# Attention's entry of a diffusion backbone step: first value tiles unit by unit, the exp table loaded ahead, background products three block steps later, and a later spread in one norm chain

## The chip, the cores and the metric

One NeuronCore of a Trainium2 chip runs the whole program. The metric is the device time of one execution in microseconds (us). The engines in the text are PE (TensorE, the matmuls), DVE (VectorE), ACT (ScalarE), POOL (GpSimd) and SP, which issues most of the DMAs.

## The reference, cut to what matters

Two layers work on 640 tokens of width 1024: 512 latent tokens and 128 context tokens. Each layer is a half-step SwiGLU FFN, a token mixer and another half-step FFN. The mixer of layer 0 is a Fourier mix, that of layer 1 is 16-head attention. Every sub-layer has an RMS norm in front and one behind, with shift, scale and gate from a modulation product.

```python
def _rmsnorm(x, g):
    x32 = x.astype(jnp.float32)
    y = x32 * lax.rsqrt(jnp.mean(x32 * x32, axis=-1, keepdims=True) + RMS_EPS)
    return (y * g.astype(jnp.float32)).astype(x.dtype)
def _modulation(cond, w_mod, b_mod):
    m = jax.nn.silu(cond) @ w_mod + b_mod
    return m.reshape(cond.shape[0], N_MOD, D_MODEL)
def _half_ffn(x, m, k, g_pre, g_post, w1, w2):
    h = _modulated_prenorm(x, g_pre, m, k)
    return x + 0.5 * m[:, 3 * k + 2, None] * _rmsnorm(_swiglu(h, w1, w2), g_post)
def _context_attention(q, k, v):
    s = jnp.einsum('bhqd,bhkd->bhqk', q, k).astype(jnp.float32)
    p = jax.nn.softmax(s, axis=-1).astype(v.dtype)
    return jnp.einsum('bhqk,bhkd->bhqd', p, v)
...
        logits = jnp.concatenate([s_loc.reshape(b, h, GRID_W, n_loc), s_ctx], axis=-1)
        p = jax.nn.softmax(logits, axis=-1).astype(v.dtype)
```

## The kernel before

Tokens lie along the free dimension and are worked in two halves of 320; channels lie on the 128 partitions in 8 chunks. The six sub-layers are numbered n = 0 to 5: FFN, Fourier mix, FFN, FFN, attention, FFN. Every product with a weight matrix is three matmuls (`mm3`, L226 to L232): each operand is split into a high and a low part, and high by high, high by low and low by high are added in one PSUM bank. A weight tile (a "unit" of 128 x 1024) is sent by one DMA into a raw buffer; ACT makes its high part (L195) and DVE its low part (L196). There are four raw buffers and six for high and low parts together.

PSUM holds four "main" banks, two "score" banks, one "turn" and one "sum" bank. The two score banks matter here: the first value tiles are accumulated in them, and the attention scores afterwards.

The order on each engine is fixed when the program is built. The code keeps a clock of its own: each `mm3` advances it (`tick`, L234), and side chains (norms, the residual additions) are generators that yield a delay and are resumed when that clock has passed it. `behind_of` (L219) and `high_priority` move an instruction in the builder's order. Each engine then works in its order; what the semaphores hold back holds back all that is behind it on that engine.

A norm chain (`inverse_rms`, L454) adds the two squares (L461, DVE), takes the mean over the channels on PE (L470), adds eps on DVE (L474), takes the power -1/2 on POOL (L475), yields `root` (2200), and spreads the result over the partitions on PE (L480); ACT copies that from PSUM. `pre` (L490) then multiplies (L505), applies shift and scale (L511 on DVE, L513 on ACT) and splits the result into the two parts of the hidden tile.

Attention's entry (`attention`, L1087 to L1104) runs while the norm of the second half is still in its chain. It takes the products of the first half (two queries, two keys), then the first two value tiles of head quad 1 and of quad 0, then the products of the second half. A value tile is 8 chunks of 3 matmuls with 256 columns; a quad has two weight units, `v0` for chunks 0 to 3 and `v1` for chunks 4 to 7. `v_tiles` (L1031) finishes one token tile before it begins the next; `v_out` (L1027) copies each finished bank to two value buffers on DVE.

`attend` (L1131) makes a list of 40 block steps, plus two to drain, that are woven into the products. One step holds the scores of a block (L1154 on PE, then one DVE instruction that adds the bias and takes the extreme, L1157, then the exponential with its sum on ACT, L1140, and a reciprocal on DVE, L1141), the scaling of the block before (L1174, ACT), its transposes (L1181, PE) and copies (L1183, ACT), and the product with the values of the one before that (L1197, PE). At every third step from 0 to 33 it also takes one job from the background: a DMA of 512 KB of the modulation matrix, and two weighted sums of it on DVE (`gemv`, L389).

Of the kernel before, what the change touches and what calls it, by code (L numbers as in the profile page):

```python
# [14 lines left out]
AF = mybir.ActivationFunctionType  # L15
# [5 lines left out]
NCH = D // P  # L21
# [89 lines left out]
class Kernel:  # L111
# [378 lines left out]
    def pre(self, layer, sub, half, acc=None, fold=1800):  # L490

        nc = self.nc
        n = layer * 3 + sub
        h = self.hs[n]
        if acc is None:
            for c in range(0, NCH, 2):
                acc = self.sum_square(acc, self.xpair(n, c, half))
        r = yield from self.inverse_rms(acc, fold=fold)
        self.normed[half][1] = True
        rb = r[:, :HALF].unsqueeze(1)  # L500
        high = self.tc.high_priority
        for c in range(0, NCH, 2):
            with high() if c == 0 else ExitStack():
                t = self.pair(self.y, c, half)
                nc.vector.tensor_tensor(t, self.xpair(n, c, half), rb.to_broadcast([P, 2, HALF]), op=ALU.mult)  # L505
                for i in (c, c + 1):
                    for s, e, cond in SEGS[half]:
                        k = self.coef[:, layer, sub, :, cond, i : i + 1]
                        t = self.y[:, i, s:e]
                        if i % 2:  # L510
                            nc.vector.tensor_scalar(t, t, k[:, 1], k[:, 0], op0=ALU.mult, op1=ALU.add)  # L511
                        else:
                            nc.scalar.activation(t, t, AF.Identity, bias=k[:, 0], scale=k[:, 1])  # L513
                self.ready = self.split(h.at(0, c, half, 2), h.at(1, c, half, 2), self.pair(self.y, c, half))
            yield 2200
# [431 lines left out]
    def attention(self, base, boundary):  # L947
        nc, io = self.nc, self.io
# [3 lines left out]
        at = {key: base + n for n, key in enumerate(QKV_ORDER)}  # L952
        early = {key: base + QKV_ORDER.index(key) for key in QKV_ORDER}
# [53 lines left out]
        def double(c):  # L1007

            with self.tc.high_priority():
                for p0, (rows, other) in enumerate(sides):  # L1010
                    k = pairs[c][1 + p0]
                    nc.vector.tensor_copy(k[other], k[rows])
# [12 lines left out]
        def v_out(quad, t, ps):  # L1025
            for i, v in enumerate(values[quad]):
                nc.vector.tensor_copy(v[:, t, :], ps[:, i * P : (i + 1) * P])  # L1027
                if t == 4:
                    nc.sync.dma_start(out=io["v_out"][2 * quad + i], in_=v[:, t, :])

        def v_tiles(quad, ts, at=at, bank="main"):  # L1031
            if quad not in values:
                kind = ("total", "square")[quad % 2]
                values[quad] = [self.temp(kind).rearrange("p (t d) -> p t d", t=5) for _ in range(2)]
            w = [self.unit(at["v0", quad]), self.unit(at["v1", quad])]
            for t in ts:
                ps = self.bank(bank)
                for kk in range(NCH):
                    a = [self.h.tokens(part, kk, t * P, (t + 1) * P) for part in range(2)]
                    ww = w[kk // 4]  # L1040
                    ws = slice((kk % 4) * 256, (kk % 4) * 256 + 256)
                    self.mm3(ps[:, :256], a[0], a[1], ww[0][:, ws], ww[1][:, ws], kk == 0, kk == NCH - 1)
                v_out(quad, t, ps)

        def products(jobs, half=None):


            todo = []
            for job in jobs:
                if job[0] == "v":  # L1050
                    quad, t = job[1:]
                    todo.append((self.bank("score"), [self.unit(early["v0", quad]), self.unit(early["v1", quad])], t))
                else:
                    todo.append((self.bank(), self.unit(early[job]), None))
            for k in range(NCH):
                for ps, w, t in todo:
                    if t is None:
                        a = k * P
                        self.mm3(ps[:, :HALF], w[0][:, a : a + P], w[1][:, a : a + P], *self.h.chunk(k, half),
                                 k == 0, k == NCH - 1)  # L1060
                    else:
                        a = [self.h.tokens(part, k, t * P, (t + 1) * P) for part in range(2)]
                        ws = slice((k % 4) * 256, (k % 4) * 256 + 256)
                        self.mm3(ps[:, :256], *a, w[k // 4][0][:, ws], w[k // 4][1][:, ws], k == 0, k == NCH - 1)

            def put(part=slice(None)):
                with self.tc.high_priority():
                    for job, (ps, w, t) in list(zip(jobs, todo))[part]:
                        if t is None:
                            {"q": query, "k": key}[job[0]](job[1], half, ps)  # L1070
                        else:
                            v_out(job[1], t, ps)
            return put
# [8 lines left out]
        for quad in (1, 0):  # L1082
            while not self.normed[1][1 - quad]:
                self.step(1)
            if quad == 0:
                with self.behind_of(self.summed, self.squared):
                    put(slice(2))  # L1087
            v_tiles(quad, (0, 1), early, "score")
        self.finish(1)
        with self.behind_of(*self.ready):  # L1090
            for c in (0, 1):
# [1 line left out]
            put(slice(2, 4))  # L1093
        with self.behind_of(self.latest):
            put = products([("k", 0), ("q", 0), ("v", 0, 3), ("v", 0, 4)], 1)
        put(slice(1))
        double(0)
        put(slice(1, None))
        v_tiles(0, (2,), early, "score")
        plan = {0: (1, (2, 3, 4)), 2: (2, (0, 1)), 3: (2, (2, 3, 4)), 4: (3, (0, 1)), 5: (3, (2, 3, 4))}  # L1100
        for c in range(NCH - 1):
            quad, ts = plan.get(c, (0, ()))
            self.weave(period(c), (qk_ns if c else qk_ns / 2) + len(ts) * v_ns)
            if c in (3, 5):  # L1104
                v_tiles(quad, ts)
            if c:
                qk(c + 1)
            else:
                for which, put in (("k", key), ("q", query)):
                    ps = self.proj(self.unit(early[which, 1]), lambda kk: kk * P, 1)  # L1110
                    with self.tc.high_priority():
                        put(1, 1, ps)
                    if which == "k":
                        double(1)
            if ts and c not in (3, 5):
                v_tiles(quad, ts)
            self.flush()
# [13 lines left out]
    def attend(self, pairs, ctx_qk, v):  # L1131
# [3 lines left out]
        nc, io = self.nc, self.io  # L1135
# [72 lines left out]
        for n in range(len(blocks) + 2):  # L1208
            parts = []
            if 1 <= n <= len(blocks):  # L1210
                parts.append(partial(scale, *blocks[n - 1]))
            if n < len(blocks):
                c, b = blocks[n]
                parts += [partial(ctx_scores if b == "c" else scores, c, b, p0) for p0 in range(2)]
            if n >= 2:
                parts.append(partial(take, *blocks[n - 2]))
            if 1 <= n <= len(blocks):
                parts += [partial(turn, *blocks[n - 1], p0) for p0 in range(2)]
            if n < 35 and n % 3 == 0:
                parts.append(self.behind)  # L1220
            steps.append(parts)
        return steps
# [143 lines left out]
```

## Time and profile before

| What | us |
|---|---|
| time, median of 3 runs (lowest to highest) | 2284.67 (2283.75 to 2285.11) |
| the profiled execution's own time | 2284.21 |
| its span | 2282.4 |
| PE busy in it | 2246.8 |
| DVE busy in it | 1731.9 |
| ACT busy in it | 1270.8 |

The span runs from the first instruction to the last of the profiled execution; the 1.8 us between it and that execution's time lie outside. Busy times of different engines overlap. The rows from the trace give a start time within the span, a duration, the engine, the line, the operation with its output and input, and in square brackets how long the engine had been idle and what ended that. Matmuls are pipelined: the start of one to the start of the next is what one costs.

### The profile page before, as it was taken

What the parts mean: (1) busy time and instruction counts of PE and PEld (TensorE: products, weight loads), DVE (VectorE), ACT (ScalarE), POOL (GpSimd) and SP (SyncE); (2) the same over time, 40 slices, a digit from 0 to 9 for tenths busy, and PEclk for the clock granted to TensorE, in tenths of its full rate; (3) what the DMA queues carried; (4) which work ended last, traced back from release to release, by engine and by line L of the source; (5) the groups of instructions that cost most, each with busy time, mean ns of one, the idle gap of its engine ahead of it and who ended that gap; (6) DMA issues with size and microseconds to landing.
All of it is one profiled execution on the core that took longest, in us unless ns stands there. A gap on an engine that the chain in (4) does not pass through costs nothing.

```text
span 2282.4 us, 39296 instructions
## 1 busy us (share of the span) xinstructions
PE 2246.8 (98%) x15666; PEld 2209.4 (97%) x15666; DVE 1731.9 (76%) x3009; ACT 1270.8 (56%) x2466; POOL 42.8 (2%) x64
## 2 busy tenths in 40 slices
PE   7999999999999999999999999999999999999998
PEld 5999999999999999999999999998998999999997
DVE  5889888588788887867878888587667485766674
ACT  5445545565654545556445554577778654545544
POOL 0000000000000000000000000000000000000000
PEclk8999999999999999999999999999999999999999
DMA  8244443433323433443234443424333222322322
GB/s 306 93 130 157 151 138 118 148 94 123 121 105 118 148 114 127 134 162 112 85 128 140 157 130 104 147 92 141 111 110 113 70 73 100 111 93 80 105 90 96
DMA packets 80280, 278.12 MB, mean 122 GB/s; under 512 B 8800, under 2 KB 15200, under 8 KB 79968
## 3 DMA queue, kind: packets, MB, share of 16 engines
q1 hardware_dynamic: 78736, 273.97, 36.4%
q8 instruction: 122, 2.00, 0.4%
q10 hardware_dynamic: 1360, 1.64, 0.2%
q14 instruction: 62, 0.51, 0.1%
HBM read 264.04 MB, written 11.53 MB: 121 GB/s over the span
## 4 chain that ended last, share of the span: by engine, by line
PE 96%; DVE 2%; DMA 1%; ACT 1%; issue 0%; POOL 0%; DVEq 0%; SPq 0%; ACTq 0%
PE main L229 28%; PE main L231 27%; PE main L230 27%; PE score L230 3%; PE score L229 3%; PE score L231 3%; PE sum L1197 1%; PE score L1154 1%; PE sum L470 1%; PE sum L480 1%; PE turn L1181 1%; DMA first<-in_w_mod_k 0%; PE main L1181 0%; DMA ring<-in_x 0%; DVE lo L196 0%
## 5 line engine op out<-in xcount | busy, mean ns | idle before, releaser
L229 PE MATMUL main<-ring,hi 128*128 128x320 f32 x3872 | 1206.4, 312 | 1.5 <-ACT ring L366 1.1
L231 PE MATMUL main<-ring,lo 128*128 128x320 f32 x3872 | 1198.2, 310 | 0.0
L230 PE MATMUL main<-ring,hi 128*128 128x320 f32 x3872 | 1198.0, 309 | 0.0
L229 PEld LDWEIGHTS main<-ring,hi 128*128 128x128 f32 x3872 | 727.9, 188 | 7.2 <-issue 3.3
L230 PEld LDWEIGHTS main<-ring,hi 128*128 128x128 f32 x3872 | 728.1, 188 | 0.8 <-issue 0.3
L231 PEld LDWEIGHTS main<-ring,lo 128*128 128x128 f32 x3872 | 727.9, 188 | 0.6 <-issue 0.5
L195 ACT ACTIVATE hi<-raw 128x1024 fp32r<-128x1024 f32 (+1 forms) x366 | 356.0, 974 | 434.6 <-PE main L230 354.4
L196 DVE TENSOR_TENSOR lo<-raw,hi 128x1024 fp32r<-128x1024 f32 (+1 forms) x366 | 408.9, 1118 | 143.9 <-ACT hi L195 142.6
L389 DVE SCALAR_TENSOR_TENSOR junk<-raw,wide 128x1024 bf16<-128x1024 f32 x256 | 312.9, 1222 | 20.1 <-DMA raw<-in_w_mod_t 17.3
L698 ACT ACTIVATE y<-main 128x320 f32<-128x320 f32 x318 | 135.5, 431 | 149.4 <-PE main L231 148.6
L672 ACT ACTIVATE main<-y 128x320 f32<-128x320 f32 x256 | 111.5, 439 | 39.1 <-DVE left L654 27.3
L229 PE MATMUL score<-ring,hi 128*128 128x320 f32 x416 | 128.7, 309 | 0.0
L230 PE MATMUL score<-ring,hi 128*128 128x320 f32 x416 | 128.5, 309 | 0.0
L231 PE MATMUL score<-ring,lo 128*128 128x320 f32 x416 | 128.5, 309 | 0.0
L425 DVE TENSOR_TENSOR total<-total,square 128x640 f32<-128x640 f32 x71 | 58.4, 824 | 83.3 <-ACT square L424 81.9
L196 DVE TENSOR_TENSOR lo<-sums,hi 128x1024 fp32r<-128x1024 f32 x72 | 88.0, 1222 | 42.1 <-ACT hi L195 41.2
L195 ACT ACTIVATE hi<-sums 128x1024 fp32r<-128x1024 f32 x72 | 76.3, 1060 | 33.6 <-DVE sums L181 19.3
L229 PE MATMUL main<-ring,ring 128*128 128x320 f32 x288 | 90.9, 316 | 0.0
L231 PE MATMUL main<-ring,ring 128*128 128x320 f32 x288 | 89.1, 310 | 0.0
L230 PE MATMUL main<-ring,ring 128*128 128x320 f32 x288 | 89.0, 309 | 0.0
L229 PEld LDWEIGHTS score<-ring,hi 128*128 128x128 f32 x416 | 78.1, 188 | 0.0
L230 PEld LDWEIGHTS score<-ring,hi 128*128 128x128 f32 x416 | 78.1, 188 | 0.0
(191 smaller groups left out, 2599.6 us busy)
## 6 DMA issues: line engine op xcount, KB each, us to landing
raw<-in_w SPq DMA_DIRECT2D x264, 512.0 KB, 3.6
raw<-in_w_mod_t SPq DMA_DIRECT2D x128, 512.0 KB, 4.2
raw<-in_qkv SPq DMA_DIRECT2D x26, 512.0 KB, 3.7
first<-in_w_mod_k SPq DMA_DIRECT2D x16, 512.0 KB, 9.2
spill<-ring SPq DMA_DIRECT2D x12, 640.0 KB, 3.3
ring<-spill SPq DMA_DIRECT2D x12, 640.0 KB, 7.0
raw<-in_bias SPq DMA_DIRECT2D x16, 448.0 KB, 3.4
raw<-in_four_in SPq DMA_DIRECT2D x8, 512.0 KB, 6.5
```

Of the source, the lines that this page charges most:

```text
L195: nc.scalar.activation(hi, raw[:, at], AF.Copy)
L196: nc.vector.tensor_tensor(lo, raw[:, at], hi.bitcast(F32), op=ALU.subtract)
L229: mm(out, whi, xhi, start=start, stop=False)
L230: mm(out, whi, xlo, start=False, stop=False)
L231: self.latest = mm(out, wlo, xhi, start=False, stop=stop)
L389: last = self.nc.vector.scalar_tensor_tensor(out=self.junk, in0=raw, scalar=1.0, in1=self.wide[:, cond, :], op0=ALU.mult, op1=ALU.mult, ac ...
L425: nc.vector.tensor_tensor(acc, acc, sq, op=ALU.add)
L470: nc.tensor.matmul(ps[:, j : j + 1], part[:, t : t + P], self.mean, start=i == j == 0 or len(acc) == 1, stop=i == len(acc) - 1, skip_group ...
L480: self.spread = nc.tensor.matmul(ps[:, t : t + P], col[:, j : j + 1].to_broadcast([P, P]), self.ident, start=True, stop=True)
L672: nc.scalar.activation(ps[:, :HALF], self.y[:, m, lo:hi], AF.Copy)
L698: nc.scalar.activation(self.y[:, m, lo:hi], ps[:, :HALF], AF.Copy)
L1154: nc.tensor.matmul(o, q, k[:, BLOCK_KEYS[b]], start=part == 0, stop=part == 1)
```

## The change

It has four parts. First, `pre` asks for the spread of one norm chain later: for the second half of sub-layer 3 (layer 1's first FFN) `root` is 3800 in place of 2200 of the code's own clock. Second, the first value tiles of quad 1 are taken unit by unit: chunks 0 to 3 of both token tiles, then chunks 4 to 7 of both, each `mm3` placed behind the one before it; both score banks are open meanwhile. Third, an exponential of one column, whose result nothing reads, is placed on ACT after the products of the second half, ahead of the copies that follow. Fourth, the background jobs go to block steps 3, 6, ... 36 in place of 0, 3, ... 33.

```diff
@@ pre
-        r = yield from self.inverse_rms(acc, fold=fold)
+        r = yield from self.inverse_rms(acc, 3800 if half and n == 3 else 2200, fold)
@@ v_tiles
-        def v_tiles(quad, ts, at=at, bank="main"):
+        def v_tiles(quad, ts, at=at, bank="main", by_unit=False):
...
-            for t in ts:
-                ps = self.bank(bank)
-                for kk in range(NCH):
+            pss = {}
+            for t, kks in ((t, kks) for kks in ((range(4), range(4, NCH)) if by_unit else (range(NCH),)) for t in ts):
+                ps = pss[t] = pss.get(t) or self.bank(bank)
+                for kk in kks:
...
-                    self.mm3(ps[:, :256], a[0], a[1], ww[0][:, ws], ww[1][:, ws], kk == 0, kk == NCH - 1)
-                v_out(quad, t, ps)
+                    with self.behind_of(*[self.latest] if by_unit else []):
+                        self.mm3(ps[:, :256], a[0], a[1], ww[0][:, ws], ww[1][:, ws], kk == 0, kk == NCH - 1)
+                if kk == NCH - 1:
+                    v_out(quad, t, ps)
@@ attention
-            v_tiles(quad, (0, 1), early, "score")
+            v_tiles(quad, (0, 1), early, "score", quad == 1)
...
+        with self.behind_of(*self.ready):
+            nc.scalar.activation(self.col(1), self.power[:, :1], AF.Exp)
         put(slice(1))
@@ attend
-            if n < 35 and n % 3 == 0:
+            if 2 < n < 38 and n % 3 == 0:
```

How this moves instructions is seen at three places. In the rows below an instruction is its line, its operation, output and input with buffer numbers, and the semaphores of engines that it waits for.

The first place is PE's row in the norm chain of the first part of the change (mean L470, spread L480, and matmuls of the FFN between them). Before:

```order
L470 MATMUL sum_11374<-mean,total_11260 128x1 x2
L231 MATMUL main_11425<-ring_11100,ring_11183 128x320
L229 MATMUL main_11425<-ring_11100,ring_11182 128x320
L230 MATMUL main_11425<-ring_11101,ring_11182 128x320
L231 MATMUL main_11425<-ring_11100,ring_11183 128x320
L480 MATMUL sum_11396<-ident,col_11378 128x128 [waits Pool_49]
```

After:

```order
L470 MATMUL sum_11374<-mean,total_11260 128x1 x2
L231 MATMUL main_11419<-ring_11100,ring_11183 128x320
L229 MATMUL main_11419<-ring_11100,ring_11182 128x320
L230 MATMUL main_11419<-ring_11101,ring_11182 128x320
L231 MATMUL main_11419<-ring_11100,ring_11183 128x320
L480 MATMUL sum_11426<-ident,col_11378 128x128 [waits Pool_49]
```

The spread stands behind the same four FFN matmuls in both; only numbers of buffers differ.

The second place is attention's entry, on PE, where the first value tile of quad 0 (`score_16124`) begins behind the spread of the second half's norm. Before:

```order
L480 MATMUL sum_16085<-ident,col_16065 128x128 [waits Pool_49]
L480 MATMUL sum_16085<-ident,col_16065 128x128 x2
L229 MATMUL score_16124<-hi_15876,ring_15778 128x256 [waits Activation_49]
L230 MATMUL score_16124<-lo_15877,ring_15778 128x256 [waits DVE_49]
L231 MATMUL score_16124<-hi_15876,ring_15779 128x256
```

After:

```order
L480 MATMUL sum_16085<-ident,col_16063 128x128 [waits Pool_49]
L480 MATMUL sum_16085<-ident,col_16063 128x128 x2
L229 MATMUL score_16124<-hi_15876,ring_15778 128x256 [waits DVE_49,PE_49,Activation_49]
L230 MATMUL score_16124<-lo_15877,ring_15778 128x256
L231 MATMUL score_16124<-hi_15876,ring_15779 128x256
```

The order is the same, but the first matmul of the tile now waits on three engines' semaphores and not on ACT's alone. The DVE semaphore is explained by DVE's row there (`score_16024` is the bank of quad 1's first tile, which `score_16124` takes over). Before:

```order
L1027 COPY square_16010<-score_16024 128x128
L1027 COPY square_16011<-score_16024 128x128
L474 TENSOR_SCALAR col_16065<-sum_16061 128x3
L981 SCALAR_TENSOR_TENSOR ring_15846<-main_15852,ring_15846 64x320 x2
L1000 TENSOR_TENSOR ring_15847<-main_15859,ring_15847 64x128
L1000 TENSOR_TENSOR ring_15848<-main_15859,ring_15848 64x128
L1000 TENSOR_TENSOR ring_15847<-main_15859,ring_15847 64x192
L1000 TENSOR_TENSOR ring_15848<-main_15859,ring_15848 64x192
L196 TENSOR_TENSOR lo_15877<-raw_15874,hi_15876 128x1024
L505 TENSOR_TENSOR y<-ring_15279,rms_16089 128x2x320
L196 TENSOR_TENSOR lo_16015<-raw_16012,hi_16014 128x1024
L511 TENSOR_SCALAR y<-y,coef 128x192
```

After:

```order
L474 TENSOR_SCALAR col_16063<-sum_16059 128x3
L981 SCALAR_TENSOR_TENSOR ring_15846<-main_15852,ring_15846 64x320 x2
L1000 TENSOR_TENSOR ring_15847<-main_15859,ring_15847 64x128
L1000 TENSOR_TENSOR ring_15848<-main_15859,ring_15848 64x128
L1000 TENSOR_TENSOR ring_15847<-main_15859,ring_15847 64x192
L1000 TENSOR_TENSOR ring_15848<-main_15859,ring_15848 64x192
L196 TENSOR_TENSOR lo_15877<-raw_15874,hi_15876 128x1024
L505 TENSOR_TENSOR y<-ring_15279,rms_16089 128x2x320
L196 TENSOR_TENSOR lo_16015<-raw_16012,hi_16014 128x1024
L511 TENSOR_SCALAR y<-y,coef 128x192
L511 TENSOR_SCALAR y<-y,coef 128x128
L1027 COPY square_16010<-score_16024 128x128
```

The two copies out of `score_16024` (L1027; of the changed kernel the first is the last row shown, the second stands right behind it) moved from the place ahead of the norm's L474 to the place behind the second L511.

The third place is DVE at the first attention scores (L1157 before is L1162 after; `ISA` with two outputs is the reduction that releases a score bank, the other is its read-out). Before:

```order
L1157 ISA left_16389,col_16390<-score_16386,raw_16384 128x384
L1157 ISA col_16390 128x1
L981 SCALAR_TENSOR_TENSOR ring_15849<-main_16461,ring_15849 64x128 x2
L981 SCALAR_TENSOR_TENSOR ring_15849<-main_16461,ring_15849 64x64 x2
L1157 ISA left_16403,col_16404<-score_16400,raw_16398 128x384
L1157 ISA col_16404 128x1
L389 SCALAR_TENSOR_TENSOR junk,mod<-raw_16412,wide 128x1024
L1141 RECIPROCAL col_16392<-col_16392 128x1
L1157 ISA left_16430,col_16431<-score_16427,raw_16384 128x384
```

After:

```order
L1162 ISA left_16391,col_16392<-score_16388,raw_16386 128x384
L1162 ISA col_16392 128x1
L196 TENSOR_TENSOR lo_16538<-raw_16535,hi_16537 128x1024
L981 SCALAR_TENSOR_TENSOR ring_15849<-main_16459,ring_15849 64x128 x2
L981 SCALAR_TENSOR_TENSOR ring_15849<-main_16459,ring_15849 64x64 x2
L1146 RECIPROCAL col_16394<-col_16394 128x1
L1162 ISA left_16405,col_16406<-score_16402,raw_16400 128x384
L1162 ISA col_16406 128x1
L196 TENSOR_TENSOR lo_16544<-raw_16541,hi_16543 128x1024
```

The L389 of the background job is gone, and an L196 of a weight unit stands between the first and the second reduction, with the reciprocal ahead of the second reduction, and another L196 behind it.

## Rows read from the trace of the kernel before

**Rows 1.** The head of the page and its first part: busy time and share of the span by engine.

```profile
span 2282.4 us, 39296 instructions
...
PE 2246.8 (98%) x15666; PEld 2209.4 (97%) x15666; DVE 1731.9 (76%) x3009; ACT 1270.8 (56%) x2466; POOL 42.8 (2%) x64
```

**Rows 2.** The waits of PE, grouped by what waited and for whom: us in total, times, the longest in us.

```profile
PE sum L480 <- POOL col L475: 2.1, 2, 1.2
...
PE score L230 <- DVE lo L196: 1.4, 2, 1.3
PE score L1154 <- DVE total L1027: 1.4, 1, 1.4
...
PE score L1154 <- ACT left L1140: 1.1, 1, 1.1
PE score L1154 <- DVE col L1141: 1.1, 1, 1.1
...
PE score L1154 <- DVE col L1157: 0.6, 2, 0.4
```

**Rows 3.** The timeline of PE in the norm chain of layer 1's first FFN, second half.

```profile
1083.43 0.75 PE L470 MATMUL sum<-mean,total 128*128 128x1 f32 x6
...
1084.57 0.30 PE L231 MATMUL main<-ring,ring 128*128 128x320 f32 x1
1085.81 0.93 PE L480 MATMUL sum<-ident,col 128*128 128x128 f32 x6 [0.94 <-POOL col L475]
```

**Rows 4.** The timeline of PE at attention's entry: mean, spread, and quad 0's two value tiles (48 matmuls from 1522.62 on, of which 1526.12 is the 14th), then the first product of the second half.

```profile
1519.57 0.73 PE L470 MATMUL sum<-mean,total 128*128 128x1 f32 x6
...
1522.62 0.36 PE L229 MATMUL score<-hi,ring 128*128 128x256 f32 x1
1524.24 0.39 PE L230 MATMUL score<-lo,ring 128*128 128x256 f32 x1 [1.26 <-DVE lo L196]
...
1526.12 0.38 PE L230 MATMUL score<-lo,ring 128*128 128x256 f32 x1 [0.17 <-DVE lo L196]
...
1530.41 0.31 PE L229 MATMUL main<-ring,hi 128*128 128x320 f32 x1
```

**Rows 5.** The timeline of DVE in the same stretch; the L1027 at 1518.69 are the copies of `score_16024`, those at 1526.64 the copies of quad 1's second tile.

```profile
1518.69 0.49 DVE L1027 COPY square<-score 128x128 f32<-128x128 f32 x2 [0.25 <-PE score L231]
1520.41 0.16 DVE L474 TENSOR_SCALAR col<-sum 128x3 f32<-128x3 f32 x1 [1.23 <-PE sum L470]
...
1522.96 1.23 DVE L196 TENSOR_TENSOR lo<-raw,hi 128x1024 fp32r<-128x1024 f32 x1
...
1524.84 1.22 DVE L196 TENSOR_TENSOR lo<-raw,hi 128x1024 fp32r<-128x1024 f32 x1
1525.98 0.63 DVE L511 TENSOR_SCALAR y<-y,coef 128x192 f32<-128x192 f32 x2
1526.64 0.49 DVE L1027 COPY square<-score 128x128 f32<-128x128 f32 x2
```

**Rows 6.** Busy time in six stretches: the stretch and its us, then busy us and instructions of PE, PEld, DVE, ACT and POOL, then the granted clock of TensorE as a share of the full one, the DMA share and GB/s. The first two lie at the start of the program, the next three around the first attention scores, the last at attention's entry.

```profile
24.00:28.70 4.70, 0.31 (x8) 0.00 (x0) 2.35 (x5) 2.71 (x5) 0.00 (x0) 0.78 1.02 405
28.70:40.30 11.60, 9.98 (x50) 7.79 (x51) 6.31 (x14) 6.01 (x11) 0.00 (x0) 0.50 0.95 361
1555.80:1559.30 3.50, 1.32 (x5) 0.60 (x5) 3.40 (x14) 3.49 (x7) 0.00 (x0) 0.99 0.05 14
1559.30:1562.70 3.40, 3.37 (x14) 3.17 (x14) 3.24 (x8) 3.07 (x8) 0.00 (x0) 0.50 0.38 92
1562.70:1566.10 3.40, 3.40 (x29) 2.74 (x29) 0.70 (x4) 2.03 (x7) 0.00 (x0) 1.00 0.61 222
1522.60:1526.20 3.60, 2.17 (x17) 1.76 (x15) 3.57 (x5) 2.06 (x4) 0.00 (x0) 1.00 0.27 57
```

**Rows 7.** The timeline of PE at the start of the program, the wait that ends the first of those stretches.

```profile
28.71 2.79 PE L317 MATMUL turn<-first,right 128*32 128x256 f32 x24 [4.39 <-DMA first<-in_w_mod_k]
```

**Rows 8.** The timeline of PE at the first attention scores.

```profile
1555.35 1.19 PE L1154 MATMUL score<-ring,ring 128*128 128x384 f32 x4 [1.43 <-DVE total L1027]
1557.64 0.59 PE L1154 MATMUL score<-ring,ring 128*128 128x384 f32 x2 [1.10 <-ACT left L1140]
1559.33 0.98 PE L1154 MATMUL score<-ring,ring 128*128 128x384 f32 x2 [1.09 <-DVE col L1141]
```

**Rows 9.** The timeline of DVE there: the second reduction, the background's L389, the reciprocal and the third reduction.

```profile
1556.93 0.56 DVE L1157 CUSTOM_DVE_ANT_0 left<-score,raw 128x384 f32<-128x384 f32 x1
...
1557.41 1.22 DVE L389 SCALAR_TENSOR_TENSOR junk<-raw,wide 128x1024 bf16<-128x1024 f32 x1
...
1558.56 0.16 DVE L1141 RECIPROCAL col<-col 128x1 f32<-128x1 f32 x1
1558.63 0.54 DVE L1157 CUSTOM_DVE_ANT_0 left<-score,raw 128x384 f32<-128x384 f32 x1
```

**Rows 10.** The timeline of ACT: an idle stretch in the products of the second half, and the first exponentials.

```profile
1542.11 1.06 ACT L195 ACTIVATE hi<-raw 128x1024 fp32r<-128x1024 f32 x1 [4.73 <-PE main L230]
...
1555.56 1.28 ACT L1140 ACT_TABLE_LOAD   x1
1556.85 0.61 ACT L1140 ACTIVATE left<-left,col 128x384 f32<-128x384 f32 x1
```

**Rows 11.** The timeline of PE at two later block steps.

```profile
1594.46 0.62 PE L1154 MATMUL score<-ring,ring 128*128 128x384 f32 x2 [0.41 <-DVE col L1157]
...
1598.27 0.55 PE L1181 MATMUL main<-ident,left 128*128 128x128 f32 x3 [0.25 <-ACT left L1174]
```

**Rows 12.** The DMAs of the attention's weight units between 1490 and 1600: time from issue to landing.

```profile
DMA to landing us min/median/max: 3.4/3.8/4.5
```

## The prediction

> **What bounds the kernel now.** I read the busy times by engine first, then PE's waits, then the timelines of PE, DVE and ACT where the change touches them. PE is busy for 98% of the span and DVE for 76% [rows 1]: a wait of PE that goes shortens the time by its length, one that is added lengthens it, and work on DVE or ACT costs only where PE stands behind it. PE's waits that the change could touch are few [rows 2]: 2.1 us for the power in two norm chains, 1.4 us for the low part of a value unit, and at the first scores 1.4, 1.1 and 1.1 us. So even a change that did away with all of them could give a few us of 2284, and the question is whether new waits come. 0.2% of the time is 4.6 us, about what a measurement of this kernel can tell from no change.
>
> **The change part by part.** The sum is made against the profiled execution, 2284.2 us, a span of 2282.4 and 1.8 outside it, which I leave as it is; it lies 0.5 below the median, and I add the sum to the median, 2284.7.
>
> *Spread in the norm chain.* In layer 1's first FFN the spread L480 waited 0.94 us for POOL's power [rows 3]. The larger `root` should put more matmuls ahead of it. The order shows the same four FFN matmuls between mean and spread before and after, so no other work covers the wait: 0. If the semaphores let it happen otherwise, the gain is at most the 0.94.
>
> *Value tiles unit by unit.* Before, quad 1's first tile was complete 24 matmuls before its second, and DVE copied it out at 1518.69, while it waited for the norm's mean anyway [rows 5]; the bank was free long before quad 0's first tile began in it at 1522.62 [rows 4]. Now both tiles are open until the end, and in DVE's order the copies stand behind L474, the query and key parts (L981, L1000), two L196, L505 and the L511. L474 waits for the mean of 1519.57 in both kernels, so that queue runs through at the old times: the L511 at 1525.98 take 0.63, and the two copies come where the L1027 of 1526.64 stood, and end at 1526.64 + 0.49 = 1527.1 [rows 5]. PE's first matmul of quad 0 now waits for them, from 1522.6 to about 1527.2, and all of PE's program is behind it: the 48 matmuls of quad 0, for whose banks DVE's next L1027 wait, and the products of the second half, for which ACT's and DVE's copies wait. Before, the first went at 1522.62, but the second and the fourteenth waited 1.26 and 0.17 for low parts [rows 4]; in the new order both low parts (L196, done at about 1524.2 and 1526.1, [rows 5]) are ready by 1527.2, so these waits are inside the new one. From the fourteenth, 35 matmuls took 1530.41 - 1526.12 = 4.29 us, 0.12 each [rows 4]; 48 take 5.8, so the second half's products start at 1527.2 + 5.8 = 1533.0 in place of 1530.41: **+2.6 us**. The unit that is released sooner gives nothing back, since its successor's low part stays where it was in DVE's queue. If I misread the release, the term is bounded below by taking away both waits, -1.4, and above by about 3.1, were another L1027 pair (0.49) ahead.
>
> *The clock after that wait.* At the first scores PE was busy for 1.32 of 3.50 us, and the next stretch of 3.40 us was granted 0.50, which is 1.2 in place of 2.4 GHz; the one after it had 1.00 again [rows 6]. At the start of the program, a wait of 4.39 us [rows 7] was also followed by 0.50, there for 11.6 us, but in a stretch with waits of its own [rows 6]. The 1.26 us wait at the entry left PE busy for 2.17 of 3.60 us, and the clock stayed at 1.00 [rows 6]. The waits just ahead of the fall at 1559.3 were 1.10 and 1.09 [rows 8], together half of 4.6; I take it that the clock falls once. In the half-clock stretch 14 matmuls went through in 3.40 us, in the next one 29 [rows 6]: 15 times 0.117 = 1.8 us lost. **+1.8 us**, between 0 and 3.5 (two such stretches). The Trainium skill ("TensorE: Matmul & The Clock Gate", section "HAM oscillation — how this bites in real kernels") says that a matmul stream that waits between its groups falls to the half clock and starts the next group cold; the rows at the first scores agree with it (0.50), and by the rule alone the fall here would be certain, by its absence the sum would be 1.8 less.
>
> *The exp table and the background.* At the first scores PE has two score banks, and a bank comes free with DVE's reduction: the second reduction ended at 1557.5 and PE went on at 1557.64, the third at 1559.2 and PE at 1559.33 [rows 8, 9]. The profile names ACT's L1140 for the second wait, but that exponential began at 1556.85, reads what the reduction wrote to SBUF, and holds no score bank. So the 1.28 us of table load [rows 10] are on ACT, not in front of PE. In the new order the second reduction has a low part (L196, 1.14 from its start to the next) and a reciprocal (0.07) ahead of it [rows 5, 9], since the background's DMA no longer takes a place in SP's queue and the weight units arrive sooner: the second wait grows from 1.10 to about 2.3, by 1.2. Behind it an L196 takes the place of the L389 of 1.22 [rows 9], the reciprocal is already gone, and the third wait shrinks by some 0.3. **+0.9 us**. Bounds: 0, if the weight's high part is late on ACT only as long as DVE has other work, or -1.1 if DVE's L196 does not delay the reduction and the wait goes; +2, if the unit's DMA, 3.4 to 4.5 us on its way [rows 12], holds up that L196. The dummy exponential and its load lie in ACT's idle 4.73 us before 1542.11 [rows 10], so they cost nothing; without that cover they would cost PE at most the 1.28 and 0.6 once. The Trainium skill ("ScalarE: Activation LUTs", section "What ACT_TABLE_LOAD costs") gives 1283 ns for the load and about as much again for a drain, 2.66 us in all; here the load took 1.28 and the next ACTIVATE began 0.01 behind it, so the measurement decides, and by the page's figure 1.4 us more could be saved only on ACT, which PE does not wait for.
>
> *Later block steps.* The background has one job fewer by any step until the end of the list, which is two L389 of 1.22 us off DVE while the waits of 0.41 and 0.25 at 1594.46 and 1598.27 build up [rows 11]; **-0.4 us**, between -0.66 and 0. The jobs are as many as before and finish three steps later, under products at full PE load: 0.
>
> The sum: 2.6 + 1.8 + 0.9 - 0.4 = +4.9, so 2284.7 + 4.9 = **2289.6 us**.
>
> **The rivals.**
>
> *The wait comes, the clock holds.* 2.6 + 0.9 - 0.4 = +3.1: 2287.8. For it speaks the 1.00 after the 1.26 us wait; against it that this wait is over three times as long.
>
> *The wait costs more.* Two stretches at half clock, 3.5 in place of 1.8: +6.6, 2291.3; with the late weight DMA at the first scores, 1.1 more. For it speaks the long half-clock stretch at the program's start [rows 6].
>
> *Not slower: the table was the cause at the first scores.* The profile does put the second wait down to L1140. If PE waited there for ACT, the load's 1.28 us goes from the chain, the second and third waits fall by 2.2 together, and with PE busy through there the clock's fall at 1559.3 (1.8) goes too. Then 2.6 + 1.8 - 2.2 - 1.8 - 0.4 = 0.0 against the old time, 2284.7, and with no fall at the entry 1.8 less, 2282.9. It decides if less than about 0.3 us of wait is left at each of these scores. Against it: DVE works in order, the L196 stands ahead of the reduction, and the banks come from the reductions.
>
> *The first part does not do what it says.* I have taken this as the forecast; were the spread later all the same, 0.94 would come off: 2288.7.
>
> **How the numbers follow.** Forecast (2288.4 to 2290.8) 0.52, clock holds 0.24, costs more 0.16, not slower 0.05, spread later 0.03. The bound for slower is 2289.24; of the forecast about 0.7 lies above it, and all of the costlier case: 0.36 + 0.16, slower 0.53. Faster by over 4.6 us needs the third rival and more: 0.03. The rest, 0.44, is within 0.2%. The range leaves out a little of the costlier case and nearly all of the not slower one: 2287.2 to 2291.6.
>
> **What would show it.** Right: a wait of PE of over 4 us ahead of a score L229 in attention's entry, put down to DVE's copies of a score bank (L1027), no wait of 1.26 for L196, and a granted clock of 0.50 within the next 7 us; the table load in ACT's idle time before the first scores, and PE's second wait there longer than 1.10; the wait of 0.94 at the spread unchanged. Wrong: copies that come before L505 on DVE, so that the first value tile of quad 0 starts near 1522.6, or waits at the first scores that vanish with the table load.

## The result and the profile after

The changed kernel took 2288.60 us (median of 13 runs, 2287.12 to 2292.21) against 2284.41 (13 runs, 2282.96 to 2287.17) for the kernel before: a ratio of 1.0021, 95% interval 1.0014 to 1.0028. It is 4.2 us slower; 4.9 had been forecast. The profiled execution of the changed kernel took 2290.32 us, 6.1 more than that of before, so its rows show somewhat more than the median does: eight of the 13 runs were faster.

The head of the page of the changed kernel and the first part of it, busy time by engine, answer to [rows 1]: PE's busy time is 3.1 us longer, the span 6.1.

```profile
span 2288.5 us, 39297 instructions
...
PE 2249.9 (98%) x15666; PEld 2212.3 (97%) x15666; DVE 1730.4 (76%) x3009; ACT 1271.0 (56%) x2467; POOL 41.8 (2%) x64
```

PE's waits in the changed kernel, grouped (us in all, times, longest), answer to [rows 2]:

```profile
PE score L229 <- DVE square L1027: 4.4, 1, 4.4
PE score L1159 <- ACT left L1179: 2.4, 1, 2.4
PE sum L480 <- POOL col L475: 2.1, 2, 1.2
PE score L1159 <- DVE total L1027: 1.4, 1, 1.4
```

The largest is new. The waits for POOL's power are as they were, and the waits for L196 at the entry (1.4) are gone. The spread that the first part of the change should have moved waits as long as before [rows 3]; this is its row on PE, and under it the early table load on ACT, which had nothing else to do there:

```profile
1086.31 0.93 PE L480 MATMUL sum<-ident,col 128*128 128x128 f32 x6 [0.94 <-POOL col L475]
```

```profile
1538.84 1.28 ACT L1100 ACT_TABLE_LOAD   x1
```

The timeline of PE at the entry in the changed kernel, beside [rows 4]:

```profile
1520.01 0.73 PE L470 MATMUL sum<-mean,total 128*128 128x1 f32 x6
1522.47 0.83 PE L480 MATMUL sum<-ident,col 128*128 128x128 f32 x6
1527.71 0.56 PE L229 MATMUL score<-hi,ring 128*128 128x256 f32 x1 [4.41 <-DVE square L1027]
...
1535.68 0.31 PE L229 MATMUL main<-ring,hi 128*128 128x320 f32 x1
```

And DVE's, beside [rows 5]:

```profile
1520.84 0.16 DVE L474 TENSOR_SCALAR col<-sum 128x3 f32<-128x3 f32 x1 [1.93 <-PE sum L470]
...
1526.41 0.63 DVE L511 TENSOR_SCALAR y<-y,coef 128x192 f32<-128x192 f32 x2
1527.07 0.88 DVE L1027 COPY square<-score 128x128 f32<-128x128 f32 x4
```

DVE runs through the same queue as before and comes to the copies of the score banks (L1027) last; the four follow each other by 0.2 us, and PE starts 0.15 us after the end of the second, at 1527.56. Between the mean and the first product of the second half lie 1535.68 - 1520.01 = 15.67 us, before 1530.41 - 1519.57 = 10.84: +4.83 at the entry. ("The entry took" means this distance below, from the mean L470 to the first product of the second half.) The whole span grew by 6.1: 0.44 lay ahead of that mean, where the change has nothing to do, and 0.83 behind the entry. The start of that mean scatters in the profiles of this study from 1518.3 to 1521.1, so a difference between whole spans of single profiles says little.

Stretches of the changed kernel, columns as in [rows 6]; three at the entry, three at the first scores:

```profile
1522.30:1525.70 3.40, 1.00 (x9) 0.81 (x8) 3.33 (x7) 1.80 (x3) 0.13 (x1) 1.00 0.07 7
1525.70:1532.50 6.80, 4.79 (x22) 4.82 (x23) 6.77 (x16) 4.33 (x9) 0.00 (x0) 0.50 0.40 141
1532.50:1535.90 3.40, 3.40 (x30) 3.40 (x29) 2.05 (x7) 2.10 (x6) 0.00 (x0) 0.99 0.00 0
1559.80:1563.20 3.40, 1.18 (x4) 0.59 (x4) 3.30 (x10) 3.29 (x10) 0.00 (x0) 1.00 0.22 78
1563.20:1570.00 6.80, 5.18 (x19) 4.31 (x20) 5.71 (x17) 5.40 (x14) 0.00 (x0) 0.51 0.48 156
1570.00:1573.40 3.40, 3.40 (x32) 3.09 (x32) 1.00 (x5) 1.87 (x6) 0.00 (x0) 0.99 0.43 135
```

The granted clock (1.00 is 2.4 GHz, 0.50 is 1.2) fell within the new wait; of the 6.80 us at 0.50 PE was still waiting for 2.0 and worked for 4.79. At the first scores the half clock lasted 6.80 us in place of 3.4.

PE at the first scores in the changed kernel, beside [rows 8], and under it DVE, beside [rows 9]:

```profile
1560.62 1.19 PE L1159 MATMUL score<-ring,ring 128*128 128x384 f32 x4 [1.43 <-DVE total L1027]
1564.23 0.98 PE L1159 MATMUL score<-ring,ring 128*128 128x384 f32 x2 [2.43 <-ACT left L1179]
...
1566.44 0.69 PE L1202 MATMUL sum<-right,total 128*64 128x128 f32 x2 [0.58 <-ACT right L1188]
```

```profile
1560.50 0.56 DVE L1162 CUSTOM_DVE_ANT_0 left<-score,raw 128x384 f32<-128x384 f32 x1
...
1560.99 1.22 DVE L196 TENSOR_TENSOR lo<-raw,hi 128x1024 fp32r<-128x1024 f32 x1
1562.24 1.06 DVE L981 SCALAR_TENSOR_TENSOR ring<-main,ring 64x128 fp32r<-64x128 f32 x4
1563.33 0.16 DVE L1146 RECIPROCAL col<-col 128x1 f32<-128x1 f32 x1
1563.52 0.56 DVE L1162 CUSTOM_DVE_ANT_0 left<-score,raw 128x384 f32<-128x384 f32 x1
```

The second reduction stands behind the L196 and the reciprocal, and PE goes on 0.15 us after the reduction's end (1564.08); the row names ACT's L1179, which is only what came last by the records. There is no third wait for a score bank any more. The 0.58 is another one: PE waits for ACT's copy of the transposes (L1188).

### The profile page after: what moved, and what is told of

The parts are those of the page before. It is cut to its first block, busy times and chain, and to the rows that moved or that the text cites. A ratio compares the mean times of both kernels' runs of the same rounds, so it can differ in the third digit from the quotient of the medians.

```text
span 2288.5 us, 39297 instructions
## 1 busy us (share of the span) xinstructions
PE 2249.9 (98%) x15666; PEld 2212.3 (97%) x15666; DVE 1730.4 (76%) x3009; ACT 1271.0 (56%) x2467; POOL 41.8 (2%) x64
## 4 chain that ended last, share of the span: by engine, by line
PE 96%; DMA 2%; DVE 1%; ACT 1%; issue 0%; POOL 0%; ACTq 0%; DVEq 0%
PE main L229 27%; PE main L231 27%; PE main L230 27%; PE score L229 3%; PE score L231 3%; PE score L230 3%; PE sum L1202 1%; PE score L1159 1%; DMA first<-in_w_mod_k 1%; PE sum L480 1%; PE sum L470 1%; PE turn L1186 1%; PE main L1186 0%; DVE lo L196 0%; DMA ring<-in_x 0%
## 5 line engine op out<-in xcount | busy, mean ns | idle before, releaser
L196 DVE TENSOR_TENSOR lo<-raw,hi 128x1024 fp32r<-128x1024 f32 (+1 forms) x366 | 408.3, 1116 | 146.0 <-ACT hi L195 144.4
L389 DVE SCALAR_TENSOR_TENSOR junk<-raw,wide 128x1024 bf16<-128x1024 f32 x256 | 312.6, 1221 | 17.3 <-DMA raw<-in_w_mod_t 14.5
L196 DVE TENSOR_TENSOR lo<-sums,hi 128x1024 fp32r<-128x1024 f32 x72 | 87.9, 1221 | 44.3 <-ACT hi L195 44.3
```

Source lines behind the costliest of these rows:

```text
L196: nc.vector.tensor_tensor(lo, raw[:, at], hi.bitcast(F32), op=ALU.subtract)
L389: last = self.nc.vector.scalar_tensor_tensor(out=self.junk, in0=raw, scalar=1.0, in1=self.wide[:, cond, :], op0=ALU.mult, op1=ALU.mult, ac ...
```

## The experiments

Each ran five rounds beside the kernel before; medians are of 11 runs, those of before of 27 to 33 runs in the same job (2284.53, 2284.68 and 2284.11 in the three jobs).

**e1, the value tiles one after the other.**

```diff
-            v_tiles(quad, (0, 1), early, "score", quad == 1)
+            v_tiles(quad, (0, 1), early, "score")
```

> The changed kernel with quad 1's value tiles taken one after the other again; the later spread, the early exp table and the later background stay. Theory (the copies of the score bank, queued late on DVE, cost the time at attention's entry): the wait of 4.4 us is gone, 1.26 and 0.17 for low parts are back, no stretch at half clock at the entry; the wait of about 2.4 at the first scores stays; 2284.4 + 0.6 = 2285.0, between 2284 and 2286. Rival (the background moved by three steps is the cost): as the changed kernel, 2288.6. Rival (the parts cost only together): 2284.4 with no wait over 1.2 at the first scores.

Measured: 2285.29, ratio 1.0004 (0.9995 to 1.0013). The entry took 10.83 us, as before; the wait of 2.4 at the first scores stayed. The other three parts together cost 0.8 us by the medians; the interval, -1.1 to +3.0 us, does not tell that from nothing.

**e2, the unit order alone** (the other three parts undone).

> The kernel before with the unit-by-unit value tiles alone. Theory: the wait of 4.4 us before quad 0's first value tile, a half-clock stretch behind it, together 4.8 at the entry, and the first scores as before: 2284.4 + 4.8 = 2289.2, between 2287.5 and 2290.5. Rival (background is the cost): 2284.4. Rival (the parts cost only together): under 2286.

Measured: 2289.10, ratio 1.0019 (1.0010 to 1.0028). PE's timeline has the wait:

```profile
1521.09 0.73 PE L470 MATMUL sum<-mean,total 128*128 128x1 f32 x6
...
1528.79 0.36 PE L229 MATMUL score<-hi,ring 128*128 128x256 f32 x1 [4.40 <-DVE square L1027]
...
1536.10 0.31 PE L229 MATMUL main<-ring,hi 128*128 128x320 f32 x1
```

The entry took 1536.10 - 1521.09 = 15.01 us, +4.17. By the medians this one part costs 4.6 us, as much as the whole change; without it 0.8 is left (e1). The background is therefore not the cause of the changed kernel's loss. The two do not add up to the 4.2 measured (4.57 + 0.76 = 5.33), but the difference is well within the intervals: what the other parts cost on top of the unit order is not shown.

**e9, the unit order with PE kept busy in the wait** (30 matmuls that nothing reads, added behind the spread).

```diff
+                spare = self.bank("turn")
+                last = self.spread
+                for _ in range(30):
+                    with self.behind_of(last):
+                        last = nc.tensor.matmul(spare[:, :HALF], self.h.tokens(0, 0, 0, P), self.h.chunk(0, 0)[0],
+                                                start=True, stop=True)
```

> The kernel before with the unit-by-unit value tiles alone, and 30 matmuls that nothing reads (128x320, some 4.4 us) put on PE between the spread and quad 0's first value tile, where it waits 4.4 us; they add work and take none away. Theory (2.6 us of the cost at the entry is the wait, the rest, 1.6 to 2.2, is the half clock behind it): PE is busy through the wait, the clock stays at full speed, the value tiles start no later: 2284.6 + 2.6 = 2287.2, about 2 below the run of the units alone (2289.1). Rival (the stretch behind the wait is slow for another reason, or the wait alone is the cost): 2289.1 or more.

Measured: 2287.45, ratio 1.0011 (1.0002 to 1.0020). PE's timeline, and two stretches with the granted clock (1.00 in both):

```profile
1520.86 0.73 PE L470 MATMUL sum<-mean,total 128*128 128x1 f32 x6
...
1523.90 4.64 PE L1095 MATMUL turn<-ring 128*128 128x320 f32 x30
1528.56 0.36 PE L229 MATMUL score<-hi,ring 128*128 128x256 f32 x1
...
1534.38 0.31 PE L229 MATMUL main<-ring,hi 128*128 128x320 f32 x1
```

```profile
1523.90:1528.60 4.70, 4.68 (x34) 4.45 (x32) 4.64 (x10) 2.67 (x5) 0.00 (x0) 1.00 0.38 116
1528.60:1534.30 5.70, 5.70 (x48) 5.70 (x49) 5.70 (x14) 3.57 (x8) 0.00 (x0) 1.00 0.26 76
```

The entry took 13.52 us: +2.68. The tiles began 7.70 us behind the mean, exactly as in e2, and their 48 matmuls ran in 1534.38 - 1528.56 = 5.8 us, in e2 in 1536.10 - 1528.79 = 7.3. So the lost 4.2 to 4.8 are 2.7 of waiting and 1.5 to 2.2 of half clock. More work on PE made the kernel faster: e9 is 3.3 us above the kernel before of its job, e2 4.6 above that of its own (1.6 apart by the two medians alone). The intervals of the two ratios overlap; it is the rows that decide.

**e4, the copies early on DVE** (the changed kernel, with the query and key parts of the first half at ordinary priority).

```diff
-            def put(part=slice(None)):
-                with self.tc.high_priority():
+            def put(part=slice(None), high=True):
+                with self.tc.high_priority() if high else ExitStack():
...
-                    put(slice(2))
+                    put(slice(2), False)
```

> The changed kernel with one thing altered: the query and key parts of the first half (L981, L1000) are placed at ordinary and not at high priority, so that on DVE the low part of quad 0's first unit and the copies of the score bank come right behind L474. Theory: those copies then end at about 1522.4 and PE, free at 1522.6, does not wait for them, nor for the low part (the 1.26); no half-clock stretch; 4.8 + 1.2 = 6.0 less than the changed kernel at the entry: 2282.6, between 2281.5 and 2284. Rival (two open banks or the order of units itself is the cost): at least 2287, the wait of over 4 us or a slower matmul stream stays.

Measured: 2285.23, ratio to before 1.0002 (0.9993 to 1.0011): 3.4 below the changed kernel, not 6. The entry went as expected, 1529.11 - 1519.67 = 9.44 us, 6.2 less than in the changed kernel. What was not expected lies behind it. The waits at the first scores are those of the changed kernel (1.44, 2.44 and 0.58), but the half clock lasted longer in this profile, 10.2 us in place of 6.8:

```profile
1555.82:1566.02 10.20, 7.42 (x31) 5.99 (x32) 7.82 (x25) 7.20 (x18) 0.00 (x0) 0.50 0.43 117
```

**e3, the background three steps later, alone.**

```diff
-            if n < 35 and n % 3 == 0:
+            if 2 < n < 38 and n % 3 == 0:
```

> The kernel before with the background products three steps later alone. Theory: the L196 of a weight unit ahead of the second reduction makes PE's second wait at the first scores about 1.2 longer (2.3 in place of 1.10), the third wait is shorter, and the waits of 0.4 and 0.25 some 40 us later go: +0.5, 2284.9, between 2284 and 2286. Rival (background is the cost): 2288.6. Rival (the table load was what PE waited for at the first scores): the waits there are as in the kernel before, 1.1 and 1.1.

Measured: 2287.86, ratio 1.0013 (1.0004 to 1.0022), where 2284.9 was expected: a miss of 3.0, and 2.6 above e1 of the same job, which has the early table too. ACT's, DVE's and PE's timelines show part of it:

```profile
1555.86 1.28 ACT L1140 ACT_TABLE_LOAD   x1
1557.15 0.61 ACT L1140 ACTIVATE left<-left,col 128x384 f32<-128x384 f32 x1
...
1557.77 1.04 ACT L195 ACTIVATE hi<-raw 128x1024 fp32r<-128x1024 f32 x1
```

```profile
1557.89 0.16 DVE L1141 RECIPROCAL col<-col 128x1 f32<-128x1 f32 x1 [0.35 <-ACT left L1140]
1557.97 0.54 DVE L1157 CUSTOM_DVE_ANT_0 left<-score,raw 128x384 f32<-128x384 f32 x1
...
1558.84 1.23 DVE L196 TENSOR_TENSOR lo<-raw,hi 128x1024 fp32r<-128x1024 f32 x1 [0.32 <-ACT hi L195]
```

```profile
1557.69 1.95 PE L1154 MATMUL score<-ring,ring 128*128 128x384 f32 x4 [2.24 <-DVE col L1157]
1559.97 0.90 PE L1181 MATMUL turn<-ident,left 128*128 128x128 f32 x3 [0.32 <-ACT left L1174]
```

Before, an L389 stood on DVE between the second and the third reduction [rows 9], and the load and the first exponential were over when it was done. Without it, DVE waits for the first exponential (0.35) and for the high part that ACT makes after it (0.32). PE's second wait does not come from that: it ends with the second reduction, which stands ahead of this reciprocal, and is 2.24 where e1 has 2.43. What the load delays is the scaling on ACT and with it the first transposes: 1559.97 lies 30.65 us behind the second half's first product (1529.32), and in e1 they come after 29.18 (1558.52, from 1529.34). Most of these 1.5 us PE fills with scores; at the mean of the next norm the profile of e3 is 0.6 behind that of e1 (table below). The other 2.0 of the 2.6 are not located: the profile of e3 is its fastest run, and over all eleven runs the mean granted clock was 0.9933, in e1 0.9943. The stretch at half clock was 10.3 us in e3's profile and 6.8 in e1's:

```profile
1556.50:1566.80 10.30, 8.21 (x33) 6.00 (x33) 7.10 (x22) 8.18 (x19) 0.00 (x0) 0.50 0.46 139
```

**e5, the early exponential alone** (`nc.scalar.activation(self.col(1), self.power[:, :1], AF.Exp)` behind the products of the second half, in the kernel before).

> The kernel before with the early exponential alone, so that the table load lies in the products of the second half. Theory: in the kernel before, an L389 of the background (1.22) lies on DVE between the second and the third reduction and covers the load of 1.28, so the load is not on PE's path and nothing is gained: 2284.5, within 0.7. Rival (the load was on PE's path at the first scores all along): the waits of 1.10 and 1.09 shrink by 1.3 or more in sum and less time runs at half clock: 2282.5.

Measured: 2285.47, ratio 1.0002 (0.9993 to 1.0011): nothing gained, as the theory had it. In the profile PE waits there 1.43 and 1.29 for score banks and 0.57 for the scaling ahead of the transposes, in place of 1.43, 1.10 and 1.09; a later wait for a reduction is 1.27 where the kernel before has 0.41 [rows 11]. With e3 and e1 this gives the early table's worth in medians: nothing with the background where it was, 2.6 us with the background moved. That the L389 as a cover makes the difference is argued from the order on DVE; the rows show some 0.6 us of it.

**e6, the spread really later.**

```diff
-        r = yield from self.inverse_rms(acc, fold=fold)
+        r = yield from self.inverse_rms(acc, 7000 if half and n == 3 else 2200, fold)
```

> The kernel before with root 7000 in place of 2200 in that one norm chain, so that 19 matmuls in place of 4 stand between the mean and the spread. Theory: the wait of 0.94 for POOL's power goes and nothing downstream becomes late: 2283.6. Rival (the spread's later users, L505 and the products behind them, become late by as much): 2284.5 with a new wait some us behind it.

Measured: 2285.03, ratio 1.0003 (0.9994 to 1.0012). The rival holds. PE's timeline:

```profile
1085.89 0.83 PE L480 MATMUL sum<-ident,col 128*128 128x128 f32 x6
...
1090.22 1.26 PE L229 MATMUL main<-ring,hi 128*128 128x320 f32 x4 [0.42 <-ACT ring L216]
...
1091.80 0.41 PE L230 MATMUL main<-ring,hi 128*128 128x320 f32 x1 [0.32 <-DVE ring L217]
```

The spread waits no more, but the first parts of the hidden tile, which hang on it, are 0.42 and 0.32 late. From the mean of this norm to the next L470 the profile even took longer, 1472.53 - 1082.41 = 390.1 us against 1473.12 - 1083.43 = 389.7 before.

**e7, the mended entry with the background where it was** (e4, the background at steps 0 to 33 again, root 7000).

> The kernel of the low put with the background products back at steps 0, 3, ... 33 and root 7000. Theory (the moved background costs at the first scores, the mended entry gains 1.1, the spread 0.9): the first scores as in the kernel before, 2284.5 - 1.1 - 0.9 = 2282.5, between 2281.5 and 2283.5. Rival (the cost at the first scores does not hang on where the background is taken): 2284.5.

Measured: 2284.16, ratio 1.0000 (0.9991 to 1.0008), 1.7 above what was expected. The entry took 9.45 us; the spread gave nothing (e6), and the rest is lost behind the entry, where the early table stays in: a wait of 1.40 for a reduction at a later score, as in e5, where the kernel before has 0.41.

**e8, the first reductions at high priority** (e7, with the reductions of the first four block steps in `high_priority` and the tile ahead of them in a main bank).

> The kernel before this one in the list, with the reductions of the first four block steps at high priority on DVE and the value tile ahead of them in a main and not a score bank, so that the first scores stand apart among the products of the second half. Theory (the waits at the first scores are PE waiting for DVE's reductions to free two score banks): the waits of 1.4, 1.1 and 1.1 and the half-clock stretch (1.8) go: 2282.5 - 5.4 = 2277.1, between 2276 and 2280. Rival (the waits come back at other places, as DVE has as much to do): 2281 or more.

Measured: 2283.94, ratio 0.9998 (0.9989 to 1.0006); 2277 was expected, and the rival holds. The scores stood apart among the products, and PE then waited at their transposes, 2.53 us at the first:

```profile
1557.06 0.55 PE L1187 MATMUL turn<-ident,left 128*128 128x128 f32 x3 [2.53 <-ACT left L1180]
```

**e10, the unit order and the ordinary priority alone**, and **e11, the ordinary priority alone** (the edit of e4, in the kernel before with and without the unit order).

> The kernel before with the unit-by-unit value tiles and the query and key parts of the first half at ordinary priority; no early table, no moved background, no later spread. Theory (each of the other three parts is worth nothing or less, the mended entry gains 1.1): 2284.6 - 1.1 = 2283.5, between 2282.8 and 2284.2. Rival (the gain at the entry is given back at the first scores, as in the run with the table and the old background): 2284.6.

> The kernel before with only the query and key parts of the first half at ordinary priority, the value tiles one after the other. Theory (the gain needs the unit that is released sooner: here its high part comes at 1520.8 as before, and the low part right behind some of the L981 and L1000): the wait of 1.26 shrinks to 0.5 to 1.0: 2284.6 - 0.5 = 2284.1. Rival (the priority alone does it, the order of units is worth nothing): 2283.5, as the run of both.

Measured: 2282.59 and 2282.33, both with a ratio of 0.9991 (0.9982 to 1.0000), a gain at the edge of what can be told from none. The entry took 9.44 us in e10 and 9.70 in e11, 1.4 and 1.1 less than before. In e11 the low part is nearly in time without the unit order:

```profile
1522.60 0.39 PE L230 MATMUL score<-lo,ring 128*128 128x256 f32 x1 [0.52 <-DVE lo L196]
```

The wait shrank to what was expected of it, the time by more; so the rival holds. What kept the low part back was its place on DVE behind all of L981 and L1000; the order of units adds 0.3 us at the entry and nothing in the medians. These are the fastest versions of the study, some 6 us below the changed kernel.

**What lies behind the entry.** The time from the second half's first product to the mean of the next norm, in one profile of each kernel, shows how much of the rest can be told. The half clock is that at the first scores.

| profile | background and table | behind the entry, us | half clock, us |
|---|---|---|---|
| before, e9, e11 | as before | 273.40, 273.38, 273.58 | 3.4 |
| e2, e6, e10 | as before | 274.14, 274.18, 274.23 | 6.8 |
| changed kernel, e1 | both changed | 274.10, 275.72 | 6.8 |
| e4 | both changed | 275.29 | 10.2 |
| e3 | background moved | 276.31 | 10.2 |
| e5, e7 | table early | 273.42, 275.51 | 3.4, 6.8 |

The ends of these times in the changed kernel, e1 and e4:

```profile
1809.78 0.72 PE L470 MATMUL sum<-mean,total 128*128 128x1 f32 x6
```

```profile
1805.06 0.72 PE L470 MATMUL sum<-mean,total 128*128 128x1 f32 x6
```

```profile
1804.40 0.72 PE L470 MATMUL sum<-mean,total 128*128 128x1 f32 x6
```

With background and table as before, 3.4 us more of half clock go with 0.6 to 0.9 us. With both changed three profiles differ by 1.6: e1 has a wait of 1.23 for ACT's scaling some 60 us behind the entry that the other two do not have, and e4 the longer half clock.

## Why the prediction was right, point by point

*The unit order.* The step was right as it stood: the copies at the end of DVE's queue, a wait of 4.41 where 4.6 was forecast, and +2.68 with the clock held (e9) where the sum had 2.6. e2 shows that this is the whole loss.

*The clock.* 1.8 was forecast for one half-clock stretch; 1.5 (e2) and 2.2 (the changed kernel: 4.83 - 2.68) were measured. e9 shows that the stretch is slow because PE had been idle: with PE busy through the same wait the clock stayed at 1.00. The forecast took the size from the first scores; that the two profiles fall on either side of it is partly luck, since the length of the stretch varies.

*The table and the background.* The forecast of +0.9 put the L196 and the reciprocal ahead of the second reduction, and the rows show just that: the second wait is 2.43 where 2.3 was expected. The third was forecast at 0.8 for a reduction and did not come; the 0.58 in its place is for ACT's copy of the transposes, so that its size fits by luck. The term also left out that the half clock would last longer there. The parts other than the unit order cost 0.8 by the medians (e1, from -1.1 to +3.0) where 0.9 - 0.4 = 0.5 stood in the sum; the profiles give 0.7 (the changed kernel) to 2.3 (e1) for them behind the entry.

One reason in this step was too narrow, though the sum did not show it: that the load is not in front of PE. It held for the kernel before (e5). But the L389 behind which it ended there is the work that the fourth part moves away, and with the background moved the kernel without the early load is 2.6 us slower than the one with it (e3 against e1), of which the rows show 0.6. The prediction had named the cover of the new place of the load, and not that of the old one.

*Later block steps.* The waits of 0.41 and 0.25 [rows 11] are not in the changed kernel, as forecast.

*The later spread.* It did not move and cost nothing, as the order said. That it would be worth 0.94 if it moved was wrong: e6 gained nothing, and 0.42 and 0.32 came back as waits.

*The rivals.* The clock did not hold; the table was not the cause at the first scores before; and the costlier case did not come.

What stays open is the price of the other three parts, nearer than some 0.7 to 2.3 us. The length of the half clock at the first scores differs between the profiles (3.4 to 10.3 us), with background and table as before 3.4 us more of it went with 0.6 to 0.9, and one profile of each kernel does not tell its part from that of the waits. Why the half clock ends sooner in one profile than in another was not tested.

## What to carry to other kernels

An accumulator bank is free when its copy has run, and on an engine that works in order the copy runs when everything placed ahead of it has (here 4.4 us of waiting): a reordering on PE must be followed to the place where the copies land on DVE, before it is costed. Where a low part or a release comes late, look first at what stands in front of it on its engine: here a lower priority of two other operations gained 1.1 us at the entry, and the reordering that was made for it 0.3 more. And work that may cover a fixed cost (the L389 over the table load) belongs to that cost's price: before it is moved, look at what would then stand in front.

## What the runs showed of the hardware

Matmuls that nothing reads made a kernel faster: 30 of them in a wait of 4.4 us kept the granted clock at 1.00, and the 48 matmuls behind it took 5.8 us (e9) in place of 7.3 (e2). The price of the same wait varies: the half clock lasted 6.80 us in the profile of the changed kernel, where it began 2.0 us before the wait ended, and 3.40 in that of e2, where it began 0.3 us after:

```profile
1529.10:1532.50 3.40, 3.40 (x19) 3.40 (x18) 3.40 (x8) 1.92 (x4) 0.00 (x0) 0.50 0.37 124
```

The changed kernel's runs scatter from 2287.12 to 2292.21, those of before from 2282.96 to 2287.17. The clock has a part in it: of the changed kernel's runs the six with a mean granted clock of 0.994 took 2287.12 to 2288.60, the seven with 0.992 or 0.993 took 2288.03 to 2292.21. That it makes the whole scatter was not shown.
